# Hymba layer on one core: output projection's halves normed at the input, gates in float32 ahead of the GLU, first feed-forward pair reordered

## The chip, the cores and the metric

The kernel runs on one core of a Trainium2 chip. The metric is device time in microseconds of one execution. TensorE (PE) does the matrix products, VectorE (DVE), ScalarE (ACT) and GpSimd (POOL) the element-wise work, SyncE (SP) issues the DMAs. Each engine runs its own queue in order and waits for the others by semaphores.

## The reference, cut to what matters

One layer for 1024 prompt positions and 8 single decode tokens (1032 columns in all), model width 1024, all in float32. The parts that the change touches:

```
xc   = conv(lru_x)                                   # 512 channels, 8 heads of 64
r, i = sigmoid(xc @ wa + ba), sigmoid(xc @ wx + bx)  # block-diagonal gates
a    = exp(8 * r * log_sigmoid(lam));  mult = sqrt(-expm1(2 * log_a))
lru_out = linear_scan(a, mult * (i * xc)) * gelu(lru_gate)
za, zb  = split(gelu(y) @ w_glu)                     # y: output of the S5 states
s5_out  = za * sigmoid(zb)
merged  = concat(rmsnorm(lru_out, g_lru_out), rmsnorm(s5_out, g_s5_out))
x32 = x + g1 * (merged @ w_out)
hn2 = rmsnorm(x32, norm2_g) * (1 + sc2) + sh2
ffn = (silu(hn2 @ w_gate) * (hn2 @ w_up)) @ w_down
x32 = x32 + g2 * ffn;   y = rmsnorm(x32, final_norm_g)
```

## The kernel before, in words

Channels lie on the 128 partitions and positions on the free axis. A float32 value that feeds a product is split into a high and a low part (`split`: ACT copies the high part, DVE or POOL subtracts to get the low one), and a product is three matmuls, high by high, high by low, low by high (`mm3`, lines 142 to 144). The weights are loaded into `wf_` tiles and split into `wh_` and `wl_`. Projections run over three column blocks of 344 (c = 0 to 2), the output projection over four of 258, and a feed-forward product takes 258 columns.

The order on PE is the order of the code. ACT's is too, from the start of the GLU part up to `ordered.close()`; elsewhere, and on DVE, POOL and SP, a scheduler at build time sets the order. Five PSUM banks (`acc_bank`) take turns for the accumulations, two small ones hold norm sums (`pc_`) and their spreads over the partitions (`pb_`), and one more is `ada_bank`.

After the input projection (`in11` is its last block, and `gt` the LRU's gate branch, to which ACT's GELU is applied at lines 1016 and 1018) the GELU outputs of S5 come back from DRAM as `gy` and are split (`gyh`, `gyl`, lines 971 to 974). Then:

- GLU block 0 (`zb`, `za`, result `s5o0`), then the gates of the LRU: for m = 0 to 3, r and i by three column blocks with split `xc` and split gate weights (`wabh`, `wabl`), 72 matmuls.
- GLU blocks 1 to 3, with the decay (`al`, exp), the tanh of `r` and the sums of squares of `s5o` (`sqs`) beside them.
- The output projection's S5 half: 8 row blocks m by 4 column blocks c, each unit 12 matmuls into a bank of its own (`os`). The norm's factor `rb_s` is applied to the result, by DVE into an `oa` tile, which POOL adds to the residual `xz`. The scans of the LRU (`lru_scan`) run beside it, then the LRU half (`ol`) runs in the same way, 12 matmuls a unit, with `rb_l`.
- The columns are kept in two halves, z = 0 and z = 1: blocks c of even and of odd number. Once the LRU units of c = 0 and 2 are done, the second norm of z = 0 is taken (`rstd_half`, `norm2_all`: `pc_n2a`, `rb_a`, the blocks `b0_`), and of z = 1 (`n2b`, `rb_b`, `b1_`) when all are done.
- The feed-forward, by pairs of 256 hidden channels, gate and up, each product by a 7-product Strassen form (X, Y, Z are its accumulators; weights A, S, T, D are sums of the raw quarters, split as `wh_g0A`, `wl_u0T` and so on). A product has 84 matmuls for each z. Pair 0 runs gate z = 0, gate z = 1, then up for both; the norm of z = 1 is taken within gate z = 0.

Norm sums go by ones-matmul on PE, then ACT (sqrt), DVE (reciprocal, cast, subtract), PE (spread), and ACT (copy to `rb_`).

Of the kernel before, what the change touches and what calls it, by code (L numbers as in the profile page):

```python
# [54 lines left out]
def body(ctx, tc, a, o):  # L55
# [1132 lines left out]
    w_glu[2] = load_w(a["w_glu"][2], "glu2")
    for m in range(4):
        lru_exp(m)  # L1190
    def half_part(h, tiles, m, lo=0, hi=TT):


        nm, cc, x = h["name"], slice(lo, hi), tiles[m]
        if m == len(h["hh"]):
            h["hh"].append(f(f"h{nm}{m}", TT, F32R))
            h["hl"].append(h["low"](f"hl{nm}{m}", TT, F32R))
# [8 lines left out]
    def half_rb(r, name, al):
        rb = al(f"rb_{name}", TT)
        rstd_spread(r, name, rb)
        grb = cp.tile([P, DK, 8], F32, tag="grb", bufs=2, name=f"grb_{name}")
# [587 lines left out]
```

## Time and profile before

| | us |
|---|---|
| median of 3 runs | 1186.59 (1186.54 to 1187.01) |
| the profiled execution | 1188.73 |
| its span | 1187.0 |
| PE busy | 1092.7 (92%) |
| DVE busy | 871.4 (73%) |
| POOL busy | 548.7 (46%) |
| ACT busy | 502.5 (42%) |
| mean granted clock of PE | 0.958 |

The busy times are sums over the span, and stages differ: a share says little about one stage. The granted clock is given as a share of full speed (2.4 GHz); 0.50 is the lower level (1.2 GHz). In a timeline a row's mark in brackets is the idle time of its engine before it and what ended that; "x3" are three instructions that the view puts together.

### The profile page before, as it was taken

To read this page: it belongs to the slowest core of one execution; us is meant where nothing else is said; L and a number is where in the kernel's file an instruction comes from. 1 tells how busy PE (TensorE), PEld (TensorE's weight loads), DVE (VectorE), ACT (ScalarE), POOL (GpSimd) and SP (SyncE) were. 2 spreads that over 40 slices of the span, in tenths; PEclk is the share of its full clock that TensorE was granted. 3 is DMA by queue.
4 is the path that set the end of the run, shared out by engine and by line. 5 is a ranking of instruction groups with operands and counts; after the bars stand their busy time and mean duration, and the time that the engine had idled before them with its cause. 6 is when DMAs were issued, how large, how long until landed. Compare 5 with 4: busy or idle time off the path is not lost.

```text
span 1187.0 us, 21442 instructions
## 1 busy us (share of the span) xinstructions
PE 1092.7 (92%) x8392; PEld 1049.6 (88%) x8392; DVE 871.4 (73%) x1394; ACT 502.5 (42%) x960; POOL 548.7 (46%) x558
## 2 busy tenths in 40 slices
PE   8887988999997985699999999999999999999995
PEld 5776877898987974599999999999999999999995
DVE  6889799844779688857866776687645357788966
ACT  4432423348743253645544445455344431121253
POOL 3397636202169758236654755475532133233022
PEclk9899989998998997799999999999999999999997
DMA  9465546341225113014532443344222977458212
GB/s 343 171 196 177 166 142 180 124 130 37 77 67 163 37 55 123 2 63 171 197 142 91 179 179 121 112 179 165 115 79 72 339 287 268 174 220 278 97 43 102
DMA packets 90341, 173.89 MB, mean 146 GB/s; under 512 B 18688, under 2 KB 54272, under 8 KB 90240
## 3 DMA queue, kind: packets, MB, share of 16 engines
q1 hardware_dynamic: 90240, 172.52, 41.3%
q8 instruction: 66, 1.08, 0.4%
q14 instruction: 35, 0.29, 0.1%
HBM read 125.51 MB, written 46.98 MB: 145 GB/s over the span
## 4 chain that ended last, share of the span: by engine, by line
PE 68%; DVE 16%; POOL 5%; issue 4%; DMA 4%; ACT 3%; SPq 1%; DVEq 0%; POOLq 0%; ACTq 0%
PE X L1464 9%; PE X L1465 9%; PE X L1466 9%; PE Y L1464 5%; PE Y L1466 5%; PE Y L1465 5%; PE Z L1464 2%; PE Z L1465 2%; PE Z L1466 2%; POOL xz L69 2%; DVE rw L69 1%; DVE xt L69 1%; DVE vt L920 1%; DVE b L69 1%; DVE acc L69 1%
## 5 line engine op out<-in xcount | busy, mean ns | idle before, releaser
L69 POOL TENSOR_TENSOR u<-u,p 128x258 f32<-128x258 f32 x44 | 39.5, 899 | 129.9 <-ACT u L1519 129.9
L142 PE MATMUL in<-hnh,wh_in 128*128 128x344 f32 (+1 forms) x240 | 82.2, 343 | 0.0
L143 PE MATMUL in<-hnl,wh_in 128*128 128x344 f32 (+1 forms) x240 | 78.8, 328 | 0.0
L144 PE MATMUL in<-hnh,wl_in 128*128 128x344 f32 (+1 forms) x240 | 78.7, 328 | 0.0
L69 POOL TENSOR_TENSOR st_d<-wf_d 128x256 f32<-128x256 f32 x32 | 24.6, 789 | 114.2 <-DMA wf_d<-w_dn 44.0
L69 POOL TENSOR_TENSOR xz<-xz,oa 128x258 f32<-128x258 f32 x64 | 66.0, 1052 | 18.2 <-DVE oa L87 15.9
L69 DVE TENSOR_TENSOR acc<-X,acc 128x258 f32<-128x258 f32 x128 | 49.8, 418 | 10.2 <-PE X L1466 10.0
L142 PEld LDWEIGHTS in<-hnh,wh_in 128*128 128x128 f32 x240 | 47.3, 197 | 2.9 <-issue 2.9
L1519 ACT ACTIVATE u<-X 128x258 f32<-128x258 f32 x88 | 33.2, 382 | 37.0 <-PE X L1466 37.0
L142 PE MATMUL ol<-hl,wh_ol 128*128 128x258 f32 x128 | 38.7, 302 | 10.5 <-DVE oa L87 5.9
L69 DVE TENSOR_TENSOR hs<-v,hs 128x516 fp32r<-128x516 f32 x32 | 47.1, 1491 | 0.7 <-ACT hs L1335 0.7
L143 PEld LDWEIGHTS in<-hnl,wh_in 128*128 128x128 f32 x240 | 47.1, 196 | 0.0
L142 PE MATMUL os<-hs,wh_os 128*128 128x258 f32 x128 | 38.3, 299 | 9.2 <-DVE oa L69 6.5
L144 PEld LDWEIGHTS in<-hnh,wl_in 128*128 128x128 f32 x240 | 46.7, 195 | 0.0
L69 POOL TENSOR_TENSOR acc<-acc,rbf 128x388 f32<-128x388 f32 x10 | 11.8, 1212 | 63.3 <-ACT rbf L204 63.3
L144 PE MATMUL os<-hs,wl_os 128*128 128x258 f32 x128 | 37.4, 292 | 1.0 <-POOL wl_os L69 1.0
L143 PE MATMUL ol<-hll,wh_ol 128*128 128x258 f32 x128 | 37.8, 295 | 0.0
L144 PE MATMUL ol<-hl,wl_ol 128*128 128x258 f32 x128 | 37.7, 295 | 0.0
L143 PE MATMUL os<-hls,wh_os 128*128 128x258 f32 x128 | 37.4, 292 | 0.0
L142 PEld LDWEIGHTS ol<-hl,wh_ol 128*128 128x128 f32 x128 | 25.8, 202 | 12.4 <-DVE oa L87 6.6
L69 POOL TENSOR_TENSOR v<-u 128x516 f32<-128x516 f32 x16 | 20.7, 1292 | 34.6 <-DVE u L69 34.6
L142 PEld LDWEIGHTS os<-hs,wh_os 128*128 128x128 f32 x128 | 25.4, 198 | 10.8 <-issue 7.2
(1621 smaller groups left out, 4915.2 us busy)
## 6 DMA issues: line engine op xcount, KB each, us to landing
ht<-hs SPq DMA_DIRECT2D x48, 516.0 KB, 3.1
db<-ht SPq DMA_DIRECT2D x48, 516.0 KB, 8.8
ad<-ada SPq DMA_DIRECT2D x48, 512.0 KB, 6.2
wf_g<-w_gu SPq DMA_DIRECT2D x22, 512.0 KB, 3.4
wf_u<-w_gu SPq DMA_DIRECT2D x22, 512.0 KB, 3.2
wf_d<-w_dn SPq DMA_DIRECT2D x16, 512.0 KB, 4.8
wf_in<-w_in SPq DMA_DIRECT2D x10, 512.0 KB, 3.6
x<-xt SPq DMA_DIRECT2D x8, 516.0 KB, 8.0
```

Source lines behind the costliest of these rows:

```text
L69: (e or V).tensor_tensor(out=out, in0=x, in1=y, op=op)
L142: PE.matmul(ps, lhsT=wh, rhs=xh, start=first, stop=False)
L143: PE.matmul(ps, lhsT=wh, rhs=xl, start=False, stop=False)
L144: PE.matmul(ps, lhsT=wl, rhs=xh, start=False, stop=last)
L920: V.tensor_tensor_scan(out=vt[:, ri, q, 8:136], data0=mag8[:, q0 + q:q0 + q + 1].to_broadcast([P, P]), data1=w[ri][:, q], initial=0.0, op0 ...
L1464: PE.matmul(b, lhsT=wh, rhs=xh, start=first and k == 0, stop=False, skip_group_check=True)
L1465: PE.matmul(b, lhsT=wh, rhs=xl, start=False, stop=False, skip_group_check=True)
L1466: PE.matmul(b, lhsT=wl, rhs=xh, start=False, stop=k == nk - 1, skip_group_check=True)
L1519: S.activation(k[name], b[bank], AF.Copy)
```

## The change

- The gates take `xc` and the gate weights in float32 as they are, one matmul instead of three, and run ahead of GLU block 0. All splits for them are gone.
- exp and tanh run for m = 0, 1 behind GLU block 0 and for m = 2, 3 behind block 1. The four scans stand behind block 2. POOL does the squares `asq`.
- The LRU half and the S5 half of the output projection are multiplied by their norm factors at the input (`half_norm`), by column half z, and split then. Both halves add up in one bank, 24 matmuls a unit, and one DVE instruction adds the result to `xz`. All units of z = 0 come first, then those of z = 1; of the first six units the LRU half runs ahead of the S5 norm's spread.
- The squares for the second norm are taken by tile of 1032 columns; the norm of z = 0 is taken beside the units of z = 1.
- Pair 0 runs gate z = 0, up z = 0, up z = 1, gate z = 1; the gate's weights are loaded and prepared a second time (`g0b`). The norm of z = 1 is taken within gate z = 0, as before.

```diff
     def lru_gates(m):
-        xh, xl = xcs[m]
...
                 b = acc_bank(f"{nm}{m}_{c}")
-                mm3(b, (wabh[:, wi_, m], wabl[:, wi_, m]), cols((xh, xl), c), True, True)
+                PE.matmul(b, lhsT=wabf[:, wi_, m], rhs=xc[m][:, c * CW:(c + 1) * CW], start=True, stop=True)
...
-    w_glu = {0: w_glu0}
-    for c in range(NC):
-        glu(0, w_glu[0], c)
-    with tc.issue_after(gy_ins[-3]):
-        w_glu[1] = load_w(a["w_glu"][1], "glu1")
-    for m in range(4):
-        lru_gates(m)
...
+    w_glu = {0: w_glu0}
+    for m in range(4):
+        lru_gates(m)
+    w_glu[1] = load_w(a["w_glu"][1], "glu1")
+    for c in range(NC):
+        glu(0, w_glu[0], c)
...
+    for c in range(NC):
+        glu(2, w_glu[2], c)
+        if c == 0:
+            half_square(hs5, 1)
+    for m in range(4):
+        lru_scan(m)
...
+    def half_norm(h, z, e=None):
+
+        for k in range(4):
...
+            stt(x, x, h["gain"][:, k:k + 1], ALU.mult, zview(h["rb"], z), ALU.mult)
+            S.activation(hh, x, AF.Copy)
+            sub(hl, x, hh.bitcast(F32), e)
+
+    def out_add(b, m, c):
+
+        blk = xblock(m, c)
+        n = min(CH, T - c * CH)
+        stt(blk[:, 0:n], b[:, 0:n], mod[:, 0, m, 0:1], ALU.mult, blk[:, 0:n], ALU.add)
         if n < CH:
-            mul(t[:, n:CH], b[:, n:CH], grb[:, m])
-        add(xblock(m, c), xblock(m, c), t, G)
...
+    r_l = half_rb(hlr)
+    rstd_spread(r_l, "l", hlr["rb"])
+    half_norm(hlr, 0)
+    x_load(0)
+    r_s = half_rb(hs5)
+    ordered_units = [[(m, z + 2 * j) for m in ms for j in range(2)] for z, ms in ((0, range(8)), (1, (6, 7, 0, 1, 2, 3, 4, 5)))]
+    AHEAD = 6
...
+        for k in range(4):
+            (wh, wl), xh, xl = wcols(w, k), *(h[n][z][k // 2][:, 2 * (k % 2) + j] for n in ("hh", "hl"))
+            PE.matmul(b, lhsT=wh, rhs=xh, start=half == 0 and k == 0, stop=False)
+            PE.matmul(b, lhsT=wh, rhs=xl, start=False, stop=False)
+            PE.matmul(b, lhsT=wl, rhs=xh, start=False, stop=half == 1 and k == 3)
...
+    for m, c in u0[:AHEAD]:
+        half_part(m, c, 0)
+    rstd_spread(r_s, "s", hs5["rb"])
+    half_norm(hs5, 0)
     for mp in range(4):
...
+        if mp > 1:
+            out_weights(0, mp)
+        out_weights(1, mp)
+    half_norm(hlr, 1)
+    half_norm(hs5, 1)
...
+    for z in range(2):
+        if z:
+            x_load(1)
+        for i, (m, c) in enumerate(ordered_units[z]):
+            if z or i >= AHEAD:
+                half_part(m, c, 0)
+            half_part(m, c, 1)
+            out_add(ubank[m, c], m, c)
+            if i % 4 == 3:
+                out_done(z, m // 2, i // 4)
+            if z and i == 1:
                 ra = rstd_half(0, "n2a")
-            if c == 1 and m == 4:
+            if z and i == 4:
                 norm2_all(0, ra)
...
+    g_w = gu_weights(0)
+    u_w = gu_weights(1)
+    gate_up(u_first, g_w, gate(u_first), order=ONE[0],
+            hooks={(1, 0): [lambda: rb_.append(rstd_half(1, "n2b"))], (4, 0): [lambda: norm2_all(1, rb_[0])]})
+    gate_up(u_first, u_w, up(u_first), order=ONE[0])
+    g_w = gu_weights(0, "b")
+    gate_up(u_first, u_w, up_first, order=ONE[1])
+    nxt = gu_weights(2)
+    gate_up(u_first, g_w, gate_second, order=ONE[1])
```

The order on ACT at the gates, first of the kernel before. `gyh` are the high parts of the GLU's input, `xch` and `wabh` those of the gates' input and weights, `gt3` the last GELU of the gate branch, `r0` and `i0` the sigmoids of the gates, `s5o0` that of GLU block 0:

```order
L973 ACTIVATE gyh2_2772<-gy2_2769 128x8
L971 ACTIVATE gyh3_2781<-gy3_2778 128x1024
L973 ACTIVATE gyh3_2781<-gy3_2778 128x8
L96 ACTIVATE xch0_2884<-xc0_1458 128x1032
L96 ACTIVATE xch1_2888<-xc1_1758 128x1032
L1016 ACTIVATE gt3_2818<-gt3_2818 128x8
L96 ACTIVATE xch2_2892<-xc2_1979 128x1032
L1018 ACTIVATE gt3_2818<-gt3_2818,bias_181 128x1024
L96 ACTIVATE xch3_2896<-xc3_2215 128x1032
L96 ACTIVATE wabh_2900<-wabf_2787 128x1024
L1178 ACT_TABLE_LOAD
L1178 ACTIVATE s5o0_2904<-zb0_0_2905 128x344
```

The same place in the changed kernel:

```order
L1133 ACT_TABLE_LOAD
L1133 ACTIVATE r0_2884<-r0_0_2885,pk_92 128x344
...
L1133 ACTIVATE i0_2894<-i0_0_2895,pk_92 128x344
L971 ACTIVATE gyh3_2781<-gy3_2778 128x1024
...
L1133 ACTIVATE r1_2904<-r1_1_2908,pk_92 128x344
L1016 ACT_TABLE_LOAD
L1016 ACTIVATE gt3_2818<-gt3_2818 128x8
L1133 ACT_TABLE_LOAD
L1133 ACTIVATE r1_2904<-r1_2_2911,pk_92 128x344
L1018 ACT_TABLE_LOAD
L1018 ACTIVATE gt3_2818<-gt3_2818,bias_181 128x1024
L1133 ACT_TABLE_LOAD
L1133 ACTIVATE i1_2914<-i1_0_2915,pk_92 128x344
```

The sigmoids of the gates moved ahead of `gyh3` and of the GELU of `gt3`, and four more table loads stand between them.

The order on ACT at the norm factors of the two halves, in the changed kernel (`pc_l`, `pc_s`: norm sums; `rb_l`, `rb_s`: spread factors; `hl0`, `hl1`: high parts of the LRU half for z = 0 and 1; `wh_s0`: S5 weights of the first two row blocks):

```order
L96 ACTIVATE wh_l1_3383<-wf_l1_3381 128x1024
L1169 ACTIVATE s5o3_3299<-zb3_2_3387 128x344
L183 ACT_TABLE_LOAD
L183 ACTIVATE pc_l_3418<-pc_l_3418,epst_86 128x258
...
L204 ACTIVATE rb_l_3428<-pb_l3_3441 128x258
...
L1199 ACTIVATE hl0_2_3453<-gt3_2818 128x516
L204 ACTIVATE rb_s_3483<-pb_s0_3570 128x258
L96 ACTIVATE wh_s0_3604<-wf_s0_3602 128x1024
L204 ACTIVATE rb_s_3483<-pb_s1_3574 128x258
L204 ACTIVATE rb_s_3483<-pb_s2_3578 128x258
L96 ACTIVATE wh_s1_3610<-wf_s1_3608 128x1024
```

Before, `hs` (the S5 half without its factor) and `wh_os0` were made beside GLU block 3; now the copy of the S5 weights stands behind the first `rb_s`.

The order on DVE around the weights `wl_u0T` of the first up product, of the kernel before (`b1_`: split blocks of the norm of z = 1, `u`, `p`: sums of the products, `g1D`, `wl_u0S`: weights):

```order
L69 TENSOR_TENSOR b1_3_1_5166<-vn1_3_5157,b1_3_1_5166 128x516
L69 TENSOR_TENSOR b1_3_2_5169<-vn1_3_5157,b1_3_2_5169 128x516
L69 TENSOR_TENSOR wl_u0S_5379<-sa_u0_4968,wh_u0S_5378 128x1024
L69 TENSOR_TENSOR u21_5241<-Y1_5243,u21_5241 128x258
L69 TENSOR_TENSOR g1D_5311<-wf_g1_1_5303,g1D_5311 128x512
...
L69 TENSOR_TENSOR u0_1_4963<-p11_5346,u0_1_4963 128x258
L69 TENSOR_TENSOR wl_u0T_5441<-sb_u0_4969,wh_u0T_5440 128x1024
```

And of the changed kernel:

```order
L69 TENSOR_TENSOR b1_2_2_4859<-vn1_2_4846,b1_2_2_4859 128x516
L69 TENSOR_TENSOR b1_3_0_4875<-xz1_3_4100,b1_3_0_4875 128x516
L69 TENSOR_TENSOR b1_3_1_4878<-vn1_3_4869,b1_3_1_4878 128x516
L69 TENSOR_TENSOR b1_3_2_4881<-vn1_3_4869,b1_3_2_4881 128x516
L69 TENSOR_TENSOR wl_u0T_4979<-sb_u0_4675,wh_u0T_4978 128x1024
L69 TENSOR_TENSOR g0bD_5035<-wf_g0b_1_5027,g0bD_5035 128x512
```

In both `wl_u0T` comes behind the splits of z = 1; before, both gate products stand between them on PE, now the up product of z = 0 needs it while they are being made.

## Rows read from the trace of the kernel before

**Rows 1.** Windows: width, busy us (PE, PEld, DVE, ACT, POOL), clock, DMA share, GB/s.

```profile
270.00:280.00 10.00, 8.74 (x39) 8.69 (x39) 8.80 (x12) 7.55 (x10) 0.20 (x1) 0.66 0.06 13
...
430.00:440.00 10.00, 5.00 (x40) 4.59 (x38) 10.00 (x12) 10.00 (x19) 7.97 (x8) 1.00 0.00 1
...
490.00:500.00 10.00, 3.03 (x11) 2.30 (x11) 10.00 (x13) 5.67 (x12) 5.54 (x6) 0.50 0.00 0
...
520.00:530.00 10.00, 10.00 (x86) 10.00 (x86) 4.20 (x8) 4.16 (x8) 1.64 (x2) 1.00 0.16 55
```

**Rows 2.** Tile views: ns min/median/max, first and last start, of five tiles.

```profile
L142 PE MATMUL zb<-gyh,wh_glu x48: 313/320/488, 266.7 to 326.8; 128*128 128x344 f32 x48
...
L142 PE MATMUL r<-xch,wabh x12: 314/318/320, 283.8 to 293.3; 128*128 128x344 f32 x12
...
L142 PE MATMUL os<-hs,wh_os x128: 276/283/505, 329.2 to 393.1; 128*128 128x258 f32 x128
...
L144 PE MATMUL ol<-hl,wl_ol x128: 277/283/419, 394.4 to 458.4; 128*128 128x258 f32 x128
...
L1464 PE MATMUL X<-b,wh_g1A x8: 278/282/285, 531.2 to 533.7; 128*128 128x258 f32 x8
```

**Rows 3.** Timeline of PE in pair 0: start, duration, line, operation, count.

```profile
499.73 0.42 PE L1466 MATMUL Z<-b,wl_g0A 128*128 128x258 f32 x1
499.94 0.42 PE L1464 MATMUL Z<-b,wh_g0A 128*128 128x258 f32 x1
...
505.22 0.28 PE L1464 MATMUL Y<-b,wh_g0S 128*128 128x258 f32 x1
505.34 0.28 PE L1465 MATMUL Y<-b,wh_g0S 128*128 128x258 f32 x1
```

**Rows 4.** Timeline of PE at the S5 outputs, float32 matmuls.

```profile
240.94 0.40 PE L948 MATMUL py<-u,tm 128*128 128x136 f32 x2
241.17 0.40 PE L950 MATMUL py<-xt,ost 128*128 128x136 f32 x2
```

**Rows 5.** Timeline of ACT from the last gyh to the gates.

```profile
267.27 1.96 ACT L971 ACTIVATE gyh<-gy 128x1024 fp32r<-128x1024 f32 x1
...
273.35 1.13 ACT L1018 ACTIVATE gt<-gt,bias 128x1024 f32<-128x1024 f32 x1
...
275.34 1.04 ACT L96 ACTIVATE wabh<-wabf 128x1024 fp32r<-128x1024 f32 x1
276.40 1.28 ACT L1178 ACT_TABLE_LOAD   x1
277.70 0.46 ACT L1178 ACTIVATE s5o<-zb 128x344 f32<-128x344 f32 x1
...
284.89 1.41 ACT L1142 ACTIVATE r<-r,pk 128x344 f32<-128x344 f32 x3
```

**Rows 6.** DMA issues, 255 to 275 us: KB each, us to landing.

```profile
wf_glu<-w_glu SPq DMA_DIRECT2D x1, 512.0 KB, 4.7
```

**Rows 7.** Timeline of DVE at the scans and the gt products.

```profile
359.17 2.28 DVE L1166 TENSOR_TENSOR_SCAN r<-al,i 128x1024 f32<-128x1024 f32 x1
...
362.29 2.99 DVE L69 TENSOR_TENSOR gt<-r,gt 128x1032 f32<-128x1032 f32 x1
...
368.61 1.22 DVE L69 TENSOR_TENSOR gt<-r,gt 128x1032 f32<-128x1032 f32 x1
```

**Rows 8.** Timeline of DVE and ACT at the LRU half's norm.

```profile
394.71 1.78 DVE L184 RECIPROCAL pc_l<-pc_l 128x258 f32<-128x258 f32 x1 [0.47 <-ACT pc_l L183]
...
398.97 0.66 ACT L204 ACTIVATE rb_l<-pb_l 128x258 f32<-128x258 f32 x2 [4.29 <-PE pb_l L202]
```

**Rows 9.** Costliest groups: POOL's additions to xz (busy us, mean ns | idle before).

```profile
L69 POOL TENSOR_TENSOR xz<-xz,oa 128x258 f32<-128x258 f32 x64 | 66.0, 1052 | 18.2 <-DVE oa L87 15.9
```

**Rows 10.** Timeline of ACT and DVE around the second norm of z = 1.

```profile
480.99 0.66 ACT L1360 ACTIVATE rb_b<-pb_n 128x258 f32<-128x258 f32 x2
...
504.13 1.29 DVE L69 TENSOR_TENSOR b<-vn,b 128x516 fp32r<-128x516 f32 x2
```

More of the change, by code (lines that the diff above doesn't have):

```diff
@@ L1179, in glu, with half_square @@
         mul(t[:, cc], ba, t[:, cc])
-    w_glu = {0: w_glu0}
-    for c in range(NC):
-        glu(0, w_glu[0], c)
-    with tc.issue_after(gy_ins[-3]):
-        w_glu[1] = load_w(a["w_glu"][1], "glu1")
-    for m in range(4):
-        lru_gates(m)
[L1188 to L1197, printed above, removed]
+    def half_square(h, m, lo=0, hi=TT):
+        nm, cc, x = h["name"], slice(lo, hi), h["x"][m]
+        if m == len(h["sq"]):
@@ new lines, in x_load, with out_weights @@
+    def x_load(z):
+        for d in range(4):
+            xz[z].append(four(f(f"xz{z}_{d}", TT)))
+            for i in range(2):
+                nc.sync.dma_start(out=xz[z][d][:, 2 * i:2 * i + 2], in_=zview(a["xt"][2 * d + i], z))
+    wos = {}
+    def out_weights(half, mp, e=None):
+        pool, tags = ((fp, ("F", "F")), (fp, ("F", "F")), (hp, ("H", "H")), (wp, ("wh", "wl")))[mp]
+        wos[half, mp] = load_w(a["w_out"][half, mp], f"{'ls'[half]}{mp}", pool=pool, tags=tags, e=e)
+    hlr = dict(name="l", gain=par("gl"), home=f, small=f, x=gt, hh=[[], []], hl=[[], []], sq=[])
@@ new lines, in body @@
+    hs5 = dict(name="s", gain=par("gs"), home=h_, small=f, x=s5o, hh=[[], []], hl=[[], []], sq=[])
+    w_glu = {0: w_glu0}
[4 more added lines that the diff above has]
+        glu(0, w_glu[0], c)
+    for m in range(2):
+        lru_exp(m)
+        lru_tanh(m)
+    w_glu[2] = load_w(a["w_glu"][2], "glu2")
+    for c in range(NC):
+        glu(1, w_glu[1], c)
+        if c == 0:
+            half_square(hs5, 0)
+    for m in (2, 3):
+        lru_exp(m)
+        lru_tanh(m)
@@ new lines, in body @@
+    w_glu[3] = load_w(a["w_glu"][3], "glu3")
+    for c in range(NC):
+        glu(2, w_glu[2], c)
+        if c == 0:
+            half_square(hs5, 1)
+    for m in range(4):
+        lru_scan(m)
+    nc.sync.dma_start(out=o["o_lru"], in_=ol)
+    for c in range(NC):
+        glu(3, w_glu[3], c)
+        if c == 0:
+            half_square(hs5, 2)
+        half_square(hs5, 3, c * CW, (c + 1) * CW)
+        if c < 2:
+            half_square(hlr, 2 * c)
+            half_square(hlr, 2 * c + 1)
+        if c == 1:
+            out_weights(0, 0, G)
+            out_weights(0, 1, G)
@@ new lines, in body, with out_done @@
+    ss, sq3 = {}, {}
+    def out_done(z, d, n):
+        nc.sync.dma_start(out=xd[z][d], in_=xz[z][d])
+        fl = xz[z][d].rearrange("p b n -> p (b n)")
+        if n == 0:
+            ss[z] = f(f"ss{z}", TT)
+            S.activation(ss[z][:, 0:TT], fl, AF.Square)
+        else:
+            q = f(f"sqx{z}_{d}", TT)
+            S.activation(q, fl, AF.Square)
+            if n < 3:
+                add(ss[z][:, 0:TT], ss[z][:, 0:TT], q)
+            else:
+                sq3[z] = q
+    xd = [[dr.tile([P, 4, CH], F32, name=f"xd{z}_{d}") for d in range(4)] for z in range(2)]
@@ L1342, in rstd_half @@
         for j in range(2):
-            PE.matmul(pc[64 * j:64 * j + 64, 0:CH], lhsT=ones[:, 0:1].to_broadcast([P, 64]), rhs=ss[z + 2 * j],
-                      start=True, stop=True, tile_position=(0, 64 * j))
+            src = [four(t)[:, 2 * i + j] for t in (ss[z], sq3[z]) for i in range(2)]
+            for n, t in enumerate(src):
+                PE.matmul(pc[64 * j:64 * j + 64, 0:CH], lhsT=ones[:, 0:1].to_broadcast([P, 64]), rhs=t,
+                          start=n == 0, stop=n == 3, tile_position=(0, 64 * j))
         S.activation(pc[:, 0:CH], pc[:, 0:CH], AF.Sqrt, bias=epst, scale=1.0 / D)
@@ L1361, in norm2_all @@
         shared = None
-        for d in range(4):
+        for n, d in enumerate(range(4)):
             u = xz[z][d]
@@ L1472, in body, with gu_weights @@
     NP = NFF // 2
[L1474 removed]
+    def gu_weights(n, again=""):
         p_, j = divmod(n, 2)
[L1476 to L1477 removed]
+        name = f"{'gu'[j]}{p_}{again}"
+        r = [load_raw(a["w_gu"][2 * p_ + i, j], f"{name}_{i}") for i in range(2)]
+        return weights_of(*r, 512, name, n in (1, 2 * NP - 1))
     def dn_weights(n):
```

197 lines of the change are left out of this document (57 added, 140 removed).

## The prediction, made before the changed kernel ran

> **What bounds the kernel now.** I first lined up the instruction order of both kernels: up to the end of the input projection and from the second feed-forward pair on it is the same, so only what lies between can differ. Then I read the 10 us table of engine busy time over that stretch, the tiles that mark its ends, and last the timelines of PE, ACT and DVE where PE is idle. In the table [rows 1] PE is full at 520 to 530, inside the pairs, with the clock at 1.00, and the same code follows to the end: what shifts there shifts the end by as much. Before it PE has holes: 5.00 of 10 us busy at 430 to 440 with DVE at 10.00, 3.03 at 490 to 500 with the clock at 0.50 and DVE again full. So in this stretch the bound is the DVE work of the norms ahead of PE, and the half clock (1.2 GHz) that PE has after each wait.
>
> The markers [rows 2]: the first GLU matmul 266.7, the first gate 283.8, the first S5 unit of the output projection 329.2, its last LRU matmul 458.3, and the first product of pair 1 531.2. The stretch lasts 264.5 us. Between 283.8 and 329.2 PE does 72 split gate matmuls and three GLU blocks of 72, 288 in 45.4 us without a hole: 0.158 us each, 11.4 a block. A 258-column matmul takes 0.12 at full clock and 0.215 at half [rows 3]. PE's bare need is then 5 x 11.4 (gates and 4 GLU blocks), 768 x 0.12 = 92 for the output projection, 336 x 0.12 = 40 for pair 0 and some 3 for norm sums: 192 of 264.5. 72 us are waits and half clock; the change is worth what it does to these.
>
> **The gates ahead of the GLU.** Split work goes (72 matmuls, the copies of xc and of the gate weights). The 24 float32 matmuls that replace them have no row of their shape. The nearest are the 136-column float32 ones of the S5 outputs, starting 0.23 apart (each leaves two records) [rows 4]: 0.23 x 344/136 = 0.58 each, 13.9 us in all, against 11.4. The bounds: nothing gained by the change if they ran at the split price per product (0.47, 11.4), 27.9 at half clock.
>
> What decides is ACT. In the order it takes gyh0 to gyh2, loads the sigmoid table, does four sigmoids, gyh3, four more, and then alternates with the GELU of gt3: five table loads up to the gates' end where one stood. A load takes 1.28, the row after it starts as it ends, and the row before it had ended at its start [rows 5]. The first two gate banks are free; the three that in11 holds come free only when DVE has done gt3's rows, which stand behind gyl3, and this waits for gyh3. So the first eight matmuls share two banks, at ACT's pace.
>
> The Trainium skill ("ScalarE: Activation LUTs", What ACT_TABLE_LOAD costs) gives a switch of tables about 1.28 us and then 1.38 more for a drain, 2.66 in all, and asks that calls be batched by set, which speaks against this order. The trace agrees with the first figure (1.28) and shows no 1.38 behind it: the ACTIVATE at 277.70 starts 0.02 after the load. By the Trainium skill the four added loads would cost 10.6, by the row 5.1.
>
> ACT is done with gyh2 at 267.27 in the trace [rows 5]. Now w_glu1's load is put ahead of the last gy loads: 512 KB, 4.7 us from issue to landing [rows 6], so 0 to 4.7 later. I take 2.2: 269.5. Then, with 0.47 per sigmoid [rows 5]: table and three sigmoids with their matmuls to +2.5, the fourth +3.4, gyh3 1.96 to +5.4, four sigmoids +7.6, table, small GELU, table +10.4, one sigmoid, table +12.1, GELU of 1.13, table +14.6, 15 sigmoids at 0.44 to +21.2. That is 290.7; with some matmuls at half clock after so many short waits I take 292 for the first GLU matmul, 288 to 297 as bounds. Gates and the first GLU block then end at 303.4. Before they ended at 283.8 + 11.4 = 295.2: **+8.2**. All four GLU blocks end at 292 + 45.6 = 337.6, against 329.2: **+8.4**.
>
> **The output projection.** Before, PE went from the GLU straight into the S5 units, whose norm factor comes after the product; the LRU's scans ran beside them. Now each half is multiplied by its factor at the input, so no unit can start before the LRU norm is there. ACT takes the four square roots only behind the third GLU block (+35.2, that is 327.2). DVE then does for four m the product (1.22 too), a scan of 2.28 and a gt product of 1.22 [rows 7], 18.9, and between them four sums of squares of that length and the small rows of s5o and the scans, some 7.8: 353.9 for the sum of squares of the LRU half. Its sqrt waits behind two weight copies and a table load (356.7); from the reciprocal (1.78) over the spread matmuls to the first rb takes 4.3 in the trace [rows 8], the four rb end at 361.5; then four DVE products and four subtractions of 516 columns (0.65 each [rows 10]) with the reciprocal of pc_s between, 1.78: 368.9 with the hops. PE idles from 337.6 to about 368, 30 us, where before it had none. Bounds: 26 to 35.
>
> Six LRU half units follow (72 matmuls, the first at 0.215): 378.8. Only behind these stand the spread matmuls of the S5 factor, for which ACT's rb_s waits, and behind rb_s on ACT stands the copy wh_s0, and behind that DVE's wl_s0, the products of both column halves and the ls0 subtractions: 14 us more of PE idle, the S5 half of the first unit done at 393.4. Bounds 8 to 18. Five S5 halves, cold, to 402.8; ten units of 24 at 0.12, 431.5; sixteen units of z=1 and the norm sums, 47.1: **478.6**, against 458.5. So +20.1; the stage's bare PE work is what it was.
>
> What is gained here lies beside it: 64 POOL additions, 66.0 us of POOL [rows 9], go, and DVE's 64 results stay (now straight into xz). DVE rows that POOL stretches get shorter: the same gt product took 2.99 and 1.22 [rows 7]. My durations above are already those of the undisturbed row. The norm of z=0 now lies beside the 46 us of z=1's units; the same steps for z=1 took 23.8 [rows 10], so I cost it at nothing; were it not covered, up to 5.
>
> **Pair 0.** Before, 458.5 to 531.2 is 72.7 us for 40 us of products. Now PE starts with two products of gate z=0 (481.5), the third waits for wl_g0S, which stands behind pc_n2b's reciprocal on DVE (about 3 us with the norm's sum), gate z=0 ends at 493. Up z=0 waits 2 for wl_u0S, and does its fourth product by 500.4. The fifth needs wl_u0T, and in the order this stands on DVE behind every split of z=1's norm. In the trace rb_b to the last b is 481.65 to 505.4, 23.8 us [rows 10]; it is ready at about 490 now, so wl_u0T is done at 514: PE idles 13.6. Bounds: 14 to 27 us for the chain. Three cold products to 520.6, up z=1 and gate z=1 10.1 each: pair 1 starts at 540.8. This stretch takes 62.2 instead of 72.7 (-10.5), since half of the norm is hidden now.
>
> **Sum:** +8.4, then +11.7 to the end of the output projection, -10.5 in pair 0: **+9.6 us**. The profiled execution (1188.73, its span 1187.0) would become 1198.3; it lies 2.1 above the median 1186.59 of the three runs, so the median becomes 1196.
>
> **Rivals.**
> - *The wait in pair 0 is covered* (the other side). Place: the fifth product of up z=0. If DVE and ACT finish z=1's norm within 10 us of rb_b, nothing of the 13.6 is left, nor of the 2.3 that the cold products cost: -15.9, 1180. It decides for not slower from a chain of 14 us. For it: the trace's 23.8 hold DVE rows that POOL stretches, as the gt product in [rows 7], and POOL is freer now. Against: DVE is at 10.00 there [rows 1].
> - *The gates run at half clock to their end.* The clock before was 0.66 over 270 to 280, where PE was 8.74 of 10 us busy [rows 1]. Then the last 15 gates take 1.16 each instead of a sigmoid's 0.44: +10.8, 1207. Against: PE works most of the time in that part.
> - *Each table switch empties ACT too.* A gap as long as the load itself behind each of the four added loads would give 4 x 1.28 = +5.1, 1201. The row shows a gap of 0.02, against it. The Trainium skill's drain, named above, would be such a gap.
> - *Even.* The S5 chain (14 us) shrinks to 4.4 because the factor is spread and wh_s0 copied before the six half units are through: 1187. Against: both stand behind them in the order.
>
> **Numbers.** Forecast 54% (own range 1189 to 1203), pair-0 wait covered 20%, half clock 12%, table drain 4%, even 10%. The range 1178 to 1209 leaves out about 2 in 10, most of it below, where several chains could be short together. A measurement of this kernel can tell 0.2%, 2.4 us. Faster: the covered wait, half of what is uneven in the even case and some of the forecast's lower tail, 25%; same 7%; slower 68%.
>
> **What would show it.** In the profile after: a GLU start near 292 and five table loads before it; PE idle of about 30 us behind the last GLU matmul with DVE full; a second hole of about 14 behind the six half units; z=1's units without holes, clock 1.00; a hole of about 13 before X<-b with wl_u0T; pair 1 at about 541. The forecast is wrong if the hole behind the GLU is under 20 us, if float32 gates take far from 0.58, or if wl_u0T comes before 505.

## The result and the profile after

The changed kernel takes 1219.7 us (median of 4 runs, 1218.79 to 1221.48), before 1186.57 beside it: ratio 1.028, interval 1.0263 to 1.0298, 33 us slower. The sign was forecast with 68%; the forecast was 1196, and the time lies above the range.

The stretch that differs can be cut at three marks, as in the prediction. The tile views of after give its marks (columns as in [rows 2]): the first GLU matmul, the first LRU half unit, the first product of pair 1.

```profile
L142 PE MATMUL zb<-gyh,wh_glu x48: 313/320/582, 296.0 to 339.2; 128*128 128x344 f32 x48
...
L1303 PE MATMUL o<-hl,wh_l x128: 277/283/580, 368.0 to 483.4; 128*128 128x258 f32 x128
...
L1478 PE MATMUL X<-b,wh_g1A x8: 279/285/416, 564.7 to 567.4; 128*128 128x258 f32 x8
```

With the last `za` matmul (341.5) and the last matmul of the output projection (485.1) from the same view:

| us | before [rows 2] | after | difference | forecast |
|---|---|---|---|---|
| GLU's end | 329.0 | 341.5 | +12.5 | +8.4 |
| output projection | 129.4 | 143.6 | +14.2 | +11.7 |
| pair 0, to pair 1 | 72.8 | 79.6 | +6.8 | -10.5 |
| sum | | | +33.5 | +9.6 |

The table of [rows 1] for after, where PE is idle (width, busy us of PE, PEld, DVE, ACT, POOL, clock, DMA share, GB/s):

```profile
270.00:280.00 10.00, 7.16 (x12) 3.75 (x13) 4.90 (x9) 6.93 (x12) 0.05 (x1) 0.58 0.00 0
280.00:290.00 10.00, 6.11 (x15) 3.42 (x15) 1.72 (x3) 9.39 (x13) 0.46 (x2) 0.84 0.00 0
...
340.00:350.00 10.00, 1.76 (x12) 1.48 (x10) 10.00 (x13) 1.55 (x2) 3.57 (x3) 0.83 0.00 0
350.00:360.00 10.00, 1.09 (x8) 0.20 (x8) 7.51 (x9) 7.33 (x10) 6.30 (x3) 0.50 0.03 10
360.00:370.00 10.00, 4.37 (x17) 2.41 (x17) 7.07 (x10) 5.00 (x11) 2.97 (x2) 0.50 0.76 238
370.00:380.00 10.00, 8.09 (x45) 7.80 (x46) 6.74 (x10) 0.00 (x0) 0.00 (x0) 0.63 0.23 78
...
510.00:520.00 10.00, 1.95 (x17) 1.75 (x15) 9.31 (x23) 6.04 (x14) 9.19 (x3) 0.69 0.00 0
520.00:530.00 10.00, 0.80 (x2) 0.50 (x2) 9.49 (x7) 4.89 (x8) 9.77 (x8) 0.50 0.00 1
530.00:540.00 10.00, 8.38 (x47) 8.38 (x48) 3.88 (x6) 0.39 (x1) 1.22 (x2) 0.61 0.17 54
```

Three holes: 270 to 290 with ACT at work, DVE little used and no DMA; 340 to 360 with DVE and ACT at work, and the clock at 0.50 until 370; 510 to 530 with DVE and POOL full. What PE waited for from 330 to 566 (engine, tile and line, releaser: us in total, times, longest):

```profile
PE pc_l L181 <- DVE sql L69: 16.8, 1, 16.8
PE X L1478 <- ACT wh_u0T L96: 13.5, 1, 13.5
PE o L1304 <- DVE ls L69: 6.4, 2, 5.6
PE X L1480 <- DVE wl_u0T L69: 5.4, 1, 5.4
PE pb_l L202 <- DVE rs_l L186: 4.1, 1, 4.1
...
PE Y L1478 <- ACT p L1528: 3.2, 1, 3.2
```

The gates on ACT (start, duration, line, operation, idle before and its releaser):

```profile
270.23 1.28 ACT L1133 ACT_TABLE_LOAD   x1
271.53 0.99 ACT L1133 ACTIVATE r<-r,pk 128x344 f32<-128x344 f32 x2
273.68 0.55 ACT L1133 ACTIVATE r<-r,pk 128x344 f32<-128x344 f32 x1 [1.17 <-PE r L1132]
274.83 0.55 ACT L1133 ACTIVATE i<-i,pk 128x344 f32<-128x344 f32 x1 [0.60 <-PE i L1132]
275.27 1.93 ACT L971 ACTIVATE gyh<-gy 128x1024 fp32r<-128x1024 f32 x1
...
281.06 1.28 ACT L1016 ACT_TABLE_LOAD   x1
282.35 0.21 ACT L1016 ACTIVATE gt<-gt 128x8 f32<-128x8 f32 x1
...
286.90 1.28 ACT L1133 ACT_TABLE_LOAD   x1
288.19 1.43 ACT L1133 ACTIVATE i<-i,pk 128x344 f32<-128x344 f32 x3
```

And on PE:

```profile
273.44 3.65 PE L1132 MATMUL i<-xc,wabf 128*128 128x344 f32 x6
```

The eight gates ahead of gt3's GELU go in ones and twos, ACT waiting for PE and PE for ACT; three of them, of two records each, take 3.65 on PE, the granted clock being 0.58 over 270 to 280. Each load costs 1.28, and the next row starts 0.01 to 0.02 after its end, as in [rows 5].

The hole in pair 0, on PE, ACT, DVE and POOL in turn:

```profile
511.67 0.28 PE L1480 MATMUL Y<-b,wl_u0S 128*128 128x258 f32 x1
525.45 0.58 PE L1478 MATMUL X<-b,wh_u0T 128*128 128x258 f32 x1 [13.50 <-ACT wh_u0T L96]
...
531.62 0.58 PE L1480 MATMUL X<-b,wl_u0T 128*128 128x258 f32 x1 [5.37 <-DVE wl_u0T L69]
532.00 0.42 PE L1478 MATMUL X<-b,wh_u0T 128*128 128x258 f32 x1
...
538.51 0.28 PE L1478 MATMUL X<-b,wh_u0A 128*128 128x258 f32 x1
...
548.81 0.28 PE L1478 MATMUL X<-b,wh_g0bA 128*128 128x258 f32 x1
...
559.38 0.58 PE L1478 MATMUL Y<-b,wh_g0bT 128*128 128x258 f32 x1 [3.19 <-ACT p L1528]
```

```profile
501.71 0.66 ACT L1394 ACTIVATE rb_b<-pb_n 128x258 f32<-128x258 f32 x2
...
524.36 1.04 ACT L96 ACTIVATE wh_u0T<-sb_u 128x1024 fp32r<-128x1024 f32 x1
...
557.17 0.63 ACT L1367 ACTIVATE hs<-v 128x516 fp32r<-128x516 f32 x1 [3.42 <-DMA ht<-hs]
...
558.97 0.36 ACT L1528 ACTIVATE p<-Y 128x258 f32<-128x258 f32 x1
```

```profile
520.51 3.83 DVE L69 TENSOR_TENSOR b<-vn,b 128x516 fp32r<-128x516 f32 x3 [1.20 <-ACT b L1367]
...
525.94 3.42 DVE L69 TENSOR_TENSOR b<-vn,b 128x516 fp32r<-128x516 f32 x2
529.29 2.28 DVE L69 TENSOR_TENSOR wl_u0T<-sb_u,wh_u0T 128x1024 fp32r<-128x1024 f32 x1
```

```profile
512.16 8.38 POOL L69 TENSOR_TENSOR vn<-xz,vn 128x258 f32<-128x258 f32 x2
...
521.76 2.02 POOL L69 TENSOR_TENSOR vn<-xz,vn 128x258 f32<-128x258 f32 x2
...
528.89 1.59 POOL L69 TENSOR_TENSOR sb_g0b<-wf_g0b,sa_g0b 128x512 f32<-128x512 f32 x1
```

From rb_b's end (502.4) to the last b (529.4) are 27.0 us, where before had 23.8 [rows 10]; then wl_u0T takes 2.28. PE has done nothing but two matmuls from 511.9 to 531.6, and goes on at half clock (pitch 0.21 at 532). The three products of up z = 0 that were left end at 538.5, up z = 1 at 548.8. A second, smaller stall comes in gate z = 1: on ACT `hs` (here the split blocks of pair 0's hidden channels, not the S5 half) waits 3.42 for the store of an earlier hs buffer, p stands behind it, and PE waits 3.2 for p. POOL makes the sums for the second preparation of the gate's weights (`sa_g0b`, `sb_g0b`) from 523.8 to 530.5, beside the last splits and wl_u0T.

### The profile page after: what moved, and what is told of

The parts are those of the page before. It is cut to its first block, busy times and chain, and to the rows that moved or that the text cites. A ratio compares the mean times of both kernels' runs of the same rounds, so it can differ in the third digit from the quotient of the medians.

```text
span 1219.7 us, 21282 instructions
## 1 busy us (share of the span) xinstructions
PE 1103.3 (90%) x8392; PEld 1052.8 (86%) x8392; DVE 848.0 (70%) x1364; ACT 510.5 (42%) x953; POOL 489.3 (40%) x491
## 4 chain that ended last, share of the span: by engine, by line
PE 71%; DVE 15%; ACT 5%; DMA 3%; issue 3%; POOL 2%; SPq 0%; DVEq 0%; POOLq 0%; ACTq 0%
PE X L1478 9%; PE X L1480 9%; PE X L1479 9%; PE Y L1478 5%; PE Y L1479 5%; PE Y L1480 5%; PE o L1304 3%; PE o L1305 3%; PE o L1303 3%; PE Z L1480 2%; PE Z L1478 2%; PE Z L1479 2%; DVE rw L69 1%; DVE xt L69 1%; DVE vt L920 1%
## 5 line engine op out<-in xcount | busy, mean ns | idle before, releaser
L69 POOL TENSOR_TENSOR st_d<-wf_d 128x256 f32<-128x256 f32 x32 | 27.5, 879 | 110.0 <-PE X L1480 42.6
L1528 ACT ACTIVATE u<-X 128x258 f32<-128x258 f32 x88 | 33.1, 382 | 42.9 <-PE X L1480 42.9
L69 POOL TENSOR_TENSOR vn<-xz 128x516 f32<-128x516 f32 x6 | 8.5, 1417 | 104.6 <-ACT xz L1407 94.2
L1304 PE MATMUL o<-ls,wh_s 128*128 128x258 f32 x128 | 37.6, 294 | 6.4 <-DVE ls L69 6.4
L1304 PE MATMUL o<-ll,wh_l 128*128 128x258 f32 x128 | 37.6, 294 | 3.3 <-DVE ll L69 3.3
L1303 PE MATMUL o<-hs,wh_s 128*128 128x258 f32 x128 | 37.5, 293 | 2.6 <-ACT hs L1199 2.6
L1303 PE MATMUL o<-hl,wh_l 128*128 128x258 f32 x128 | 37.6, 293 | 0.4 <-ACT hl L1199 0.4
L1305 PE MATMUL o<-hs,wl_s 128*128 128x258 f32 x128 | 37.3, 291 | 0.0
L1305 PE MATMUL o<-hl,wl_l 128*128 128x258 f32 x128 | 37.2, 291 | 0.0
L69 DVE TENSOR_TENSOR u<-Y,u 128x258 f32<-128x258 f32 x44 | 18.7, 425 | 24.0 <-PE Y L1480 23.9
L69 DVE TENSOR_TENSOR acc<-Y,acc 128x258 f32<-128x258 f32 x64 | 26.6, 424 | 10.5 <-PE Y L1480 9.7
```

The source lines that it names most:

```text
L69: (e or V).tensor_tensor(out=out, in0=x, in1=y, op=op)
L1303: PE.matmul(b, lhsT=wh, rhs=xh, start=half == 0 and k == 0, stop=False)
L1304: PE.matmul(b, lhsT=wh, rhs=xl, start=False, stop=False)
L1305: PE.matmul(b, lhsT=wl, rhs=xh, start=False, stop=half == 1 and k == 3)
L1528: S.activation(k[name], b[bank], AF.Copy)
```

## Experiments

Each was timed against the kernel before on its own chip (4 executions each up to e7, 10 to 12 from e8 on); stages are from the profiles, by the marks above. The stages ahead of the change vary by up to 3 us from run to run, so a stage's length tells more than a mark.

| run | us | ratio to before (95%) | GLU's end | output proj. | pair 0 |
|---|---|---|---|---|---|
| changed kernel | 1219.7 | 1.0263 to 1.0298 | 341.5 | 143.6 | 79.6 |
| e1_t_early | 1210.2 | 1.0163 to 1.0220 | 339.1 | 144.6 | 69.9 |
| e2_old_pair | 1208.0 | 1.0150 to 1.0209 | 343.0 | 144.6 | 68.2 |
| e3_gates_behind | 1207.2 | 1.0144 to 1.0199 | 330.8 | 144.5 | 77.3 |
| e5_one_table | 1209.9 | 1.0155 to 1.0239 | 337.0 | 143.7 | 77.4 |
| e6_proj_alone | 1200.4 | 1.0083 to 1.0126 | 333.3 | 144.9 | 68.0 |
| e7_s_spread | 1204.9 | 1.0127 to 1.0180 | 339.0 | 135.8 | 72.3 |
| e8_before_f32 | 1191.2 | 1.0023 to 1.0048 | 330.6 | 128.6 | 74.3 |
| e9_scans_early | 1188.3 | 0.9995 to 1.0018 | 335.4 | 127.9 | 67.9 |
| e10_both_sums | 1184.6 | 0.9960 to 0.9994 | 334.1 | 125.2 | 67.5 |
| e11_hook | 1192.2 | 1.0022 to 1.0047 | 335.0 | 126.3 | 73.2 |
| e12_new_pair | 1184.9 | 0.9962 to 0.9989 | 335.2 | 125.2 | 69.2 |
| e13_hook_t | 1184.0 | 0.9967 to 0.9992 | 335.2 | 125.2 | 66.8 |

**e1_t_early.**

```diff
-            hooks={..., (4, 0): [lambda: norm2_all(1, rb_[0])]})
+            hooks={..., (4, 0): [lambda: u_w("S", 0), lambda: u_w("T", 0), lambda: norm2_all(1, rb_[0])]})
```

> The changed kernel with the S and T weights of the first up product made ahead of the norm of z=1 instead of behind it. Theory A (the splits of z=1's norm are the bound of pair 0 whatever stands in front of them; wl_u0T only adds its own length): the hole of 19.7 us before the fifth product of up z=0 goes, but one of about the same end appears before the first product of up z=1, which needs b1_: pair 1 starts at about 558 instead of 564.7, total about 1213. Theory B (the place of wl_u0T behind the norm is what costs, as the prediction had it): nearly all of the hole goes, 14 to 18 us, total about 1204.

Pair 0 takes 69.9, 9.7 less: between the two. The wait for wh_u0T is gone; what is left (483 to 556):

```profile
PE Y L1478 <- ACT p L1528: 4.9, 2, 3.1
PE X L1480 <- DVE wl_u0A L69: 4.5, 1, 4.5
```

So the weights' place behind the norm's splits cost about 10 us of the 18.9 that PE waited there. The norm is no shorter: its last split ends 46.1 us after the projection's last unit (483.7 to 529.8), against 44.3 in the changed kernel, and the 23.8 us behind it hold a stall of 3.1 at p again.

**e2_old_pair.** Pair 0 written as before, with the norm of z = 1 in the same place:

```diff
-    gate_up(u_first, g_w, gate(u_first), order=ONE[0], ...)
-    gate_up(u_first, u_w, up(u_first), order=ONE[0])
-    g_w = gu_weights(0, "b")
-    gate_up(u_first, u_w, up_first, order=ONE[1])
-    gate_up(u_first, g_w, gate_second, order=ONE[1])
+            kw = dict(order=APART, hooks=hooks) if n == 0 else ...
+            gate_up(u, get, (gate, up)[j](u), **kw)
```

> The changed kernel with pair 0 in the order of before (gate z=0, gate z=1, then up for both, gate weights prepared once). Theory A (the norm of z=1 is ready at about 529 in either order, and the products that are left then run): about 30 us of products from there, pair 1 at 558 to 564, total 1213 to 1219, no slower than the changed order. Theory B (the new order hides half of the norm and only wl_u0T spoils it): without it the stretch takes 72 us again as before, pair 1 at 558. Rival C (the new order is worth the 10 us that were forecast): slower, 1225 or more.

Pair 0 takes 68.2: the changed order costs 11.4 here. Rival C falls, and theory A's total (1213 or more) is missed too; pair 1 starts at 555.8, nearest to theory B. The total fell by as much (1219.7 to 1208.0). The old order also does without the second preparation of the gate's weights (`g_w = gu_weights(0, "b")`), which this run does not separate. The trace points at it: the last two splits on DVE are

```profile
526.04 1.29 DVE L69 TENSOR_TENSOR b<-vn,b 128x516 fp32r<-128x516 f32 x2
```

with POOL idle, where the same two took 3.42 in the changed kernel beside the sums of g0b. The last split ends 39.7 us after the projection's last unit here (487.6 to 527.3), against 44.3.

**e3_gates_behind.** The gates after GLU block 0, still float32:

```diff
+    for c in range(NC):
+        glu(0, w_glu[0], c)
+    with tc.issue_after(gy_ins[-3]):
+        w_glu[1] = load_w(a["w_glu"][1], "glu1")
     for m in range(4):
         lru_gates(m)
-    w_glu[1] = load_w(a["w_glu"][1], "glu1")
-    for c in range(NC):
-        glu(0, w_glu[0], c)
```

> The changed kernel with its float32 gates behind GLU block 0, where they stood before. Theory A (the place of the gates costs, since eight of them share two banks and ACT loads five tables while PE waits and its clock falls; the matmuls themselves cost 2.5 us): GLU ends at 331 to 334 instead of 341.5, total 1209 to 1212. Rival D (the float32 matmuls themselves are the cost): GLU ends at 338 or later, total 1217 or more.

GLU's end 330.8, 10.7 earlier; theory A, rival D falls. With the gates, w_glu1's load goes back behind the gy loads, and gyh2 is done at 267.7 instead of 270.2: up to 2.5 of the 10.7 is the place of this load. This run also shows the price of a float32 gate with PE full: 12 r gates of two records each, and as many of i (tile view, as in [rows 2]):

```profile
L1132 PE MATMUL r<-xc,wabf x24: 450/452/453, 283.0 to 294.9; 128*128 128x344 f32 x24
...
L1132 PE MATMUL i<-xc,wabf x24: 452/452/453, 284.7 to 296.6; 128*128 128x344 f32 x24
```

From the first record's start at 283.0 to the last one's at 296.6 are 13.6 us for 24 gates less one record: 13.6 / 23.5 = 0.58 each, as forecast from [rows 4].

**e5_one_table.**

```diff
-                S.activation(t[:, c * CW:(c + 1) * CW], b, AF.Sigmoid, bias=bias_[:, m:m + 1])
+                with tc.issue_after(gelus[-1]):
+                    S.activation(t[:, c * CW:(c + 1) * CW], b, AF.Sigmoid, bias=bias_[:, m:m + 1])
```

Here `gelus[-1]` is gt3's GELU.

> The changed kernel with the gates' sigmoids ordered behind the GELU of gt3 on ACT, so that one table load stands there instead of five; the place on PE is the same. Theory A1 (the table loads and the two shared banks are the cost): the sigmoids start about 276 to 278 and run without holes, GLU starts at 290 to 292 instead of 296.0, total 1214 to 1216. Rival (PE's half clock after the wait is the cost): 24 float32 matmuls at 1.16 from 272 on would end at 300, GLU starts at 296 or later, total no better than 1219.

GLU starts at 291.5, its end is 4.5 earlier: theory A1. The first sigmoid starts at 279.94, later than expected, and the 24 follow without a hole; the single matmuls at half clock did not hold them. The time (1206 to 1216) is too spread to add to this. So of the 10.7 that the gates' place costs, some 4.5 are the interleaved tables and banks, and about 6 remain in this order, the place of w_glu1's load among them.

**e6_proj_alone.** e2 and e3 together.

> The changed kernel with both other parts undone: float32 gates behind GLU block 0 and pair 0 in the order of before, so that the output projection (and the place of exp, tanh and scans) is what differs from before, besides the gates' type. If the parts add up (place of the gates 10.5, pair 0 11.3 in the runs so far): GLU ends at 331 (before 329.2), the output projection takes 143 to 144 us (before 129.4), pair 0 68 (before 72.6), total 1197 to 1199. If they hide each other: 1203 or more.

1200.4 lies between the two: above what parts that add up would give, below 1203. By the stages they nearly add up (144.9 in the output projection, 68.0 in pair 0, GLU's end 333.3 in a run whose GLU started 1.6 late). The 13.5 us that are left against the kernel before lie in the output projection, 144.9 for 129.4.

**e7_s_spread.**

```diff
-    for m, c in u0[:AHEAD]:
-        half_part(m, c, 0)
     rstd_spread(r_s, "s", hs5["rb"])
     half_norm(hs5, 0)
+    for m, c in u0[:AHEAD]:
+        half_part(m, c, 0)
```

> The changed kernel with the spread of the S5 half's factor and its products put ahead of the first six LRU half units on PE, instead of behind them. Theory (the second hole, about 13 us around 383 to 397, is there because the spread stands behind the half units): the first unit is done at about 391 instead of 397, z=1 ends at 479 to 481 instead of 485.4, total 1213 to 1216. Rival (DVE is the bound of that hole whatever the order, and the half units now start 9 us later): no gain or a loss, total 1219 or more.

The output projection takes 135.8, 7.8 less, as the theory has it (4 to 6 were expected). The total fell more than expected, because pair 0 got 7.3 shorter too: its waits for wh_u0T and wl_u0T are 10.3 and 2.2 there, against 13.5 and 5.4. Why the build's order changed that far away was not pursued.

**e8_before_f32.** Only the gates' type, in the kernel before:

```diff
-                mm3(b, (wabh[:, wi_, m], wabl[:, wi_, m]), cols((xh, xl), c), True, True)
+                PE.matmul(b, lhsT=wabf[:, wi_, m], rhs=xc[m][:, c * CW:(c + 1) * CW], start=True, stop=True)
```

> The kernel before with float32 gates at their old place, nothing else. 24 matmuls at 0.58 for 72 at 0.158 put 2.5 us on PE, which is full there: GLU ends at 331.5 to 332, total 1188 to 1190. If the splits that go (8 us of ACT and 6 of DVE ahead of GLU block 0) had held PE back: same or faster, 1183 to 1187.

Slower by 0.23 to 0.48%, 4.3 us, more than the 2.5 and above the 1188 to 1190 expected: GLU's end is 1.6 later in a run that began 1.1 early. The splits that go had been covered.

**e9_scans_early.** On top of e6, the S5 spread as in e7, and:

```diff
+    for m in range(4):
+        lru_exp(m)
     for c in range(NC):
         glu(1, w_glu[1], c)
+        if c < 2:
+            lru_tanh(2 * c)
+            lru_tanh(2 * c + 1)
...
+    for m in range(4):
+        lru_scan(m)
     for c in range(NC):
         glu(2, w_glu[2], c)
-    for m in range(4):
-        lru_scan(m)
```

Not shown: the first squares of the S5 half move behind GLU block 1 too, and the GLU's sigmoids are ordered behind gt3's GELU.

> As the run with the output projection alone, with three more edits: exp for all m behind the gates and tanh within GLU block 1 as before, the four scans behind GLU block 1 instead of 2, and the S5 factor's spread ahead of the six half units; sigmoids of the GLU behind gt3's GELU. Theory (the hole behind the GLU, 26.5 us, is the LRU chain from the square roots to its norm, so it moves with the scans): the hole shrinks to 10 to 14 us, the output projection takes 120 to 126 us, total 1174 to 1182, faster than both kernels. Rival (the norms of both halves at the input are themselves that long on DVE): hole of 20 or more, total 1190 or more.

The output projection takes 127.9, 17 less than in e6 (7.8 of it is the S5 spread's place by e7), but the total is a miss: 1188.3, the same as before. From the GLU's end to the first unit are 30.4 us, not 10 to 14, since the S5 factor is now made in that hole as well. The wait for the LRU's sums went from 16.8 to 9.0, not away, and the next one is the S5 factor (333 to 535):

```profile
PE pc_l L181 <- DVE sql L69: 9.0, 1, 9.0
PE pb_s L202 <- DVE rs_s L186: 8.2, 1, 8.2
```

The square roots among the GLU's sigmoids also hold PE now (a wait of 2.0 for s5o): GLU's end is 335.4, not 331.

**e10_both_sums.** On top of e9, both sums and spreads ahead of the products:

```diff
     r_l = half_rb(hlr)
+    r_s = half_rb(hs5)
     rstd_spread(r_l, "l", hlr["rb"])
+    rstd_spread(r_s, "s", hs5["rb"])
     half_norm(hlr, 0)
     x_load(0)
-    r_s = half_rb(hs5)
...
-    rstd_spread(r_s, "s", hs5["rb"])
     half_norm(hs5, 0)
```

> As the run with the earlier scans, with the sums, reciprocals and spreads of both halves taken one after the other ahead of any product by them, so that PE no longer waits 8.2 us for the S5 factor behind the LRU products. Theory (holes go with the place of the small steps of the norms in the queues): the LRU half units start 7 to 9 us earlier than 365.8, total 1179 to 1182, faster than before by 0.4 to 0.7%. Rival (DVE has that much to do there whatever the order): less than 3 us gained, 1185 or more.

The half units start at 356.7 instead of 365.8, and the wait for the S5 factor is 3.0 for its sums:

```profile
PE pc_s L181 <- DVE sqs L69: 3.0, 1, 3.0
```

1184.6 is faster than before by 0.06 to 0.4%, less than the 1179 to 1182 expected, and by the ratios some 3.6 us better than e9: between theory and rival. The six half units then wait 2.2 and 0.9 for ll, and run into the S5 splits.

**e11_hook.** On top of e10:

```diff
-             (4, 0): [lambda: norm2_all(1, rb_[0])]
+             (2, 0): [lambda: norm2_all(1, rb_[0])]
-            add(h["sq"][0][:, cc], h["sq"][0][:, cc], h["sq"][m][:, cc])
+            add(h["sq"][0][:, cc], h["sq"][0][:, cc], h["sq"][m][:, cc], G if h is hs5 and m < 3 else V)
```

> As the run before it in this call, with two more edits: the spread of the second norm's factor of z=1 behind the third product of gate z=0 instead of the fifth (its input was ready 6.5 us before the copies rb_b there), and the sums of squares of the S5 half for m = 1, 2 on POOL. Theory (pair 0 is bound by the chain of z=1's norm in any order): pair 0 gets 4 to 6 us shorter than 67.8, total 1174 to 1177. Rival: the products left behind the norm are the bound, no more than 2 us gained.

A miss on both accounts, slower than theory and rival had it, and the same trap as the changed kernel's: with the norm issued ahead of the fifth product of the gate, this product's weights came behind the splits.

```profile
PE X L1478 <- ACT wh_g0T L96: 21.0, 1, 21.0
PE pc_l L181 <- DVE sql L69: 11.0, 1, 11.0
```

Pair 0 grew to 73.2, and POOL's sums made the first wait longer by 2.

**e12_new_pair.** On top of e10, the changed order of pair 0 with e1's weights.

> As the first run of this call, but with pair 0 in the changed order (gate z=0, up z=0, up z=1, gate z=1, weights prepared a second time) and up's S and T weights made ahead of the norm. If the order itself hides the norm as the prediction had it, pair 0 takes 58 to 63 us and the total is 5 us or more below that run. Theory A (the norm of z=1 ends last in either order, and the second preparation and the stores add work): pair 0 takes 67 to 71 us, the total is the same or 1 to 3 us above.

69.2 against 67.5, the totals the same: theory A. Its waits:

```profile
PE Y L1478 <- ACT p L1528: 7.1, 3, 3.1
PE X L1480 <- DVE wl_u0A L69: 5.3, 1, 5.3
```

The last two splits on DVE, of e10 and then of this run:

```profile
497.39 1.29 DVE L69 TENSOR_TENSOR b<-vn,b 128x516 fp32r<-128x516 f32 x2
```

```profile
504.13 2.39 DVE L69 TENSOR_TENSOR b<-vn,b 128x516 fp32r<-128x516 f32 x2
```

The changed order does leave less behind them: 28.1 us in e10 (498.7 to 526.8) and 23.1 here (506.5 to 529.6), 3.1 of it a stall at p. But they end 39.4 us after the projection's last unit in e10 and 46.1 here, where DVE makes wl_u0S, wl_u0T and wl_u0A ahead of the splits or among them (3.8 us) and POOL the sums of g0b beside the last ones. So 5.0 us are gained and 6.7 lost; how much of the loss is the second preparation, and how much the order itself, no run separates.

**e13_hook_t.** e10 with the earlier spread, the gate's T weights first:

```diff
-             (4, 0): [lambda: norm2_all(1, rb_[0])]
+             (2, 0): [lambda: nxt_("T", 0), lambda: norm2_all(1, rb_[0])]
```

> The run with both sums taken first, with the spread of z=1's factor behind the third product of gate z=0 as in the run that got slower by it, but with the gate's T weights made ahead of the norm. Theory (that run lost its time because wh_g0T and wl_g0T came to stand behind the norm's splits on ACT and DVE, as wl_u0T does in the changed kernel): no wait for wh_g0T above 2 us, pair 0 at 64 to 66 us instead of 73 there and 67.3 without the edit, total 1180 to 1184. Rival (the earlier spread itself disturbs the stage): 1188 or more.

No wait for wh_g0T is left, pair 0 takes 66.8: the 21.0 were the weights' place. Against e10 the gain is not clear of the spread. 1184.0 is faster than before by 0.08 to 0.33%, and than the changed kernel by some 35 us.

## Why the prediction was wrong, point by point

- **The step that failed: pair 0, "-10.5, since half of the norm is hidden now".** It came out at +6.8, 17.3 of the 23.9 us by which the sum was short. The hole was named with its cause (wl_u0T behind every split of z = 1's norm) and put at 13.6; it was 19.7. From the projection's last unit to the hole's end the sum has 35.4 us (478.6 to 514), the trace 46.5 (485.1 to 531.6). The factor's rb_b came 17.3 after the last unit (11.4 taken): its spread stands behind five products on PE, of which the third waits twice 1.5 and most of what follows it runs at half clock, 494.5 to 500.1. The splits took 27.0 for 23.8. And wl_u0T, for which the sum left next to nothing (490 + 23.8 is 513.8, and it was to be done at 514), took 2.28. These make 11.1 of the 17.3. The other 6.3 lie behind the hole (33.1 for 26.8), though not where half clock had been allowed for: the three cold products took 6.9 for 6.6 and up z = 1 10.3 for 10.1, but gate z = 1 took 15.9 for 10.1, with the stall of 3.2 at p and half clock from there to its end, neither of which was in the sum.
- **Why the order gave nothing.** The forecast took the chain's length from the kernel before and moved products ahead of it. The runs show that the order changes the chain too. From the projection's last unit to the last split are 47.1 us before (458.3 to 505.4), 39.7 and 39.4 with the old order behind the new projection (e2, e10), and 44.3, 46.1 and 46.1 with the changed order (the changed kernel, e1, e12). Once the weights stand ahead of the norm, the changed order has less left behind the last split (23.1 in e12, 28.1 in e10) and loses that again in the chain: 68 to 70 us either way (e10, e2, e12, e1).
- **The gates: +8.4 forecast, +12.5 measured.** The mechanism was right in its main parts (eight gates that share two banks, five loads of 1.28, 0.58 for a float32 matmul with PE full); the GLU started at 296.0, within the bounds, 4 us later than taken. gyh2 ended at 270.2 for 269.5. The pace was not ACT's: where a sigmoid waits for its matmul two of them stand 1.15 apart (273.68 and 274.83), since the matmul ran at half clock; I had put 0.55. e3 shows that the place costs 10.7, up to 2.5 of it that of w_glu1's load, e8 that the float32 price itself is 2.7 us by the stage and 4.3 by the time.
- **The output projection: +11.7 forecast, +14.2 measured.** That it came so near is in part luck, since two errors cancel: the hole behind the GLU was 26.5 us (341.5 to 368.0) where I had 31.3 (26 to 35 as bounds), and the six LRU half units took 15.2 us, 368.0 to 383.2, where I had 9.9. They wait 3.3 for `ll` at their start and run at half clock up to 377.4 (0.63 in 370 to 380). The second hole came as described. The rest of the stage took 101.9 for 99.8. e7 shows that the second hole hangs on the spread's place, e9 and e10 that the wait for the LRU's sums moves with the scans (16.8 to 9.0).
- **The rivals.** The covered wait (1180) needed a chain of 14 us and fell: the splits took 27.0. The gates at half clock to their end (1207): only part of them were, 0.84 in 280 to 290. The drain behind each table switch (the Trainium skill, "ScalarE: Activation LUTs", What ACT_TABLE_LOAD costs) does not show in either trace: the rows at 282.35 and 288.19 start 0.01 after their loads end. "Even" needed the S5 chain down to 4.4: PE waited 0.9, 2.6 and 5.6 in it for rb_s, hs and ls alone.
- **The range** was too narrow above: I had each of three chains at its middle, and half clock in pair 0 behind the hole only, not behind the short waits. None of the three signs named for a wrong forecast came (the first hole was 26.5, the matmuls took 0.58 with PE full, wl_u0T came at 531.6): a chain that grows was not among them.

## What to carry to other kernels

Putting other products ahead of a long chain gains what it takes from the work behind the chain, less what it adds to the chain: add the two up for both orders (39.4 + 28.1 and 46.1 + 23.1 us here), and look for what the new order puts into the queues of the engines that make the chain, such as a second preparation of weights. What is put ahead must also have its own inputs ahead: twice here (wl_u0T, wh_g0T) a weight preparation of 1 to 2 us stood in an engine's queue behind some 20 us of splits, and PE with it. And price half clock behind the short waits as well as behind the holes, for as long as the nearest rows show it.

## What the runs showed of the hardware that was not expected

- After the hole of 19.7 us PE stayed at the lower level (1.2 GHz) up to 537.6, pitch 0.21 to 0.22, and the granted clock over 530 to 540 was 0.61 though PE was 8.38 of 10 us busy; after the wait of 16.8 and the short ones behind it 0.50 over 360 to 370 and 0.63 over 370 to 380. The same is seen behind short waits: after two of 1.5 the pitch was 0.215 from 494.5 to 500.1, and after the 3.2 at p from 559.4 to 564.7. Estimated from the pitches (0.215 for 0.12), these stretches of pair 0 cost 2.7, 2.4 and 2.3 us beside their waits.
- Two POOL subtractions of 258 columns took 8.38 us at 512, the same operation 2.02 for two at 521.76 in the same run. DVE worked beside both: its subtractions of 516 columns took 0.65 to 0.69 each in the first stretch, and three of them 3.83 in the second. So POOL was slow in the one and DVE in the other; what decides which, no run shows.
